# A 128-row second product in the split attention scores of a hybrid encoder kernel

## The chip, the cores and the metric

The kernel runs on one core of one Trainium2 chip. The metric is the device time of one execution in microseconds, as the median of several executions.

## The reference, cut to what matters

Two layers, each with one combined input projection whose columns feed differential attention (8 heads of two softmax maps), multi-head latent attention (8 heads) and a gate; then one output projection onto the residual. There are 512 frames and 2048 channels, all in 32-bit floats.

```python
for l in range(DEPTH):                       # DEPTH = 2
    h = _rmsnorm(x, norm_g[l])
    proj = einsum('bsd,de->bse', h, w_in[l])
    dq, dk, dv, cq, ckv, kr, gate = split(proj)
    # differential attention: for each block of 128 queries, for each map m
    #   s = q_m k_m^T * 64**-0.5 + bias ;  p = softmax(masked s)
    #   o = (p_1 - lam * p_2) v,   then an RMSNorm per head
    # latent attention: s = (q_nope k_nope^T + q_rope k_rope^T) * 192**-0.5
    y = concatenate([o_a, o_b], -1) * silu(gate)
    x = x + einsum('bse,ed->bsd', y, w_out[l])
return _rmsnorm(x, final_norm_g)
```

A block of queries reads only the keys up to its own end, so a score is 128 x w with w = 128, 256, 384 or 512.

## The kernel before, in words

Products that must keep 32-bit accuracy are made of parts. A value is split into a high part, rounded to the type fp32r that TensorE multiplies at full rate, and a low part, the rest. The projections use three products (high x high, high x low, low x high), all in `mm3` (line 249). Weights come in units of 512 KB: `emit_dma` loads one into one of two raw buffers, `emit_split` (lines 195, 196) makes the high part on ScalarE (`whi`) and the low part on VectorE (`wlo`), into four buffers each. `touch` issues the splits up to two units ahead of the unit in use.

The scores of differential attention have only 64 rows to sum over for each map. `split_stack` (lines 484, 486) therefore writes q for map m as 128 rows: the high part in the map's own half, the low part in the other half. `evac_qk` writes the high part of k into both halves and the low part of k, `kl`, into the map's own half only (lines 742 to 745). `mm_stack` then makes a score of two products: one over 128 rows with the high part of k (line 492), which gives high x high and low x high at once, and one over the 64 rows of the map's own half with the low part of k (line 493). `diff_scores` calls it for both maps of a head. `mla_scores` calls it once, behind a plain 32-bit product (line 523); its rotary key has high and low parts in both halves already, as `lat_kr` transposes a doubled copy. So in each layer 8 heads x 4 blocks x 2 maps, and 8 heads x 4 blocks, run through lines 492 and 493.

Every engine works off its instructions in the order in which the program issues them. `mix` puts the attention steps of one group of two heads (`pend`) between the projection pieces of the next group. Within a group a pipeline runs: in each slot the scores of one block, the transposes of an earlier block's probabilities (line 309, tiles `pT`), then the products with v (lines 573 and 620), each one or two slots behind. `evac_qk` stands at the end of each QK group, eight times in all. Small per-row statistics live in the pool `st`, and the low parts of k in the pool `kl`.

Of the kernel before, what the change touches and what calls it, by code (L numbers as in the profile page):

```python
# [11 lines left out]
F32 = mybir.dt.float32  # L12
F32R = mybir.dt.float32r
AF = mybir.ActivationFunctionType
ALU = mybir.AluOpType
AX = mybir.AxisListType

P = 128
S = 512
# [12 lines left out]
BUCKETS = 32  # L32
MAX_DIST = 128
MAPS = 16
# [3 lines left out]
NVEC = 640  # L38
# [16 lines left out]
def tile_hybrid_trunk(ctx, tc, x, norm_g, w_in, diff_lambda, diff_subln_g, mla_q_norm_g,  # L55
                      mla_w_q_b, mla_kv_norm_g, mla_w_kv_b, w_out, rel_bias, final_norm_g,
                      onehot, cos2, sin1, out):
    nc = tc.nc
# [4 lines left out]
    def pool(name, bufs, space=None):  # L63
        kw = {} if space is None else {"space": space}
        return ctx.enter_context(tc.tile_pool(name=name, bufs=bufs, **kw))

    const = pool("const", 1)
    big = pool("big", 16)
# [6 lines left out]
    bip = pool("bias", 2)  # L75
    tp = pool("tmp", 4)
    op = pool("o", 2)
    stp = pool("st", 16)
    keep = pool("keep", 4)
    krp = pool("kr", 1)  # L80
    klp = pool("kl", 3)
    pj = pool("pj", 4, bass.MemoryType.PSUM)
    at = pool("at", 4, bass.MemoryType.PSUM)
    dr = pool("dr", 1, bass.MemoryType.DRAM)
# [1 line left out]
    def B(shape, dtype, name):  # L86
        return big.tile(shape, dtype, tag="B", name=name)

    def T(name, pl=None, tag="T"):
        return (pl or tp).tile([P, 512], F32, tag=tag, name=name)  # L90

    def stat(name):
        return stp.tile([P, 8], F32, tag="st", name=name)

    def bank(name):
        return at.tile([P, 512], F32, tag="at", name=name)

    def acopy(out, in_, scale=1.0):
        nc.scalar.activation(out, in_, AF.Copy, scale=scale)  # L99
# [117 lines left out]
    def group(ids, nb, mm, evac, order=None, ahead=2, cost=4):  # L217

        banks = {}
        left = {u: nb for u, _, _ in ids}  # L220
        seen = dict.fromkeys(range(nb), 0)
        kt = ids[-1][1] + ids[-1][2]
        if order is None:
            order = [(i, b) for i in range(len(ids)) for b in range(nb)]

        def piece(i, b):
            u, k0, n = ids[i]
            hi, lo = touch(u, ahead)
            if b not in banks:
                banks[b] = pj.tile([P, 512], F32, tag="pj", name="pj")  # L230
            for k in range(n):
                mm(banks[b], b, hi, lo, k, k0 + k, seen[b] == 0, seen[b] == kt - 1)
                seen[b] += 1
            left[u] -= 1
            if left[u] == 0:
                finish(u)
            if seen[b] == kt:
                evac(b, banks.pop(b))

        return [(ids[i][2] * cost, lambda i=i, b=b: piece(i, b)) for i, b in order]  # L240
# [10 lines left out]
    def mm_T(act):  # L251

        def mm(bk, b, hi, lo, k, kb, first, last):
            c = slice(b * P, (b + 1) * P)
            mm3(bk, (hi[:, k, c], lo[:, k, c]), act(kb), True, first, last)
        return mm

    def mm_S(act, w):

        def mm(bk, b, hi, lo, k, kb, first, last):  # L260
            c = slice(b * P, (b + 1) * P)
            ahi, alo = act(kb)
            mm3(bk[:, :w], (hi[:, k, :w], lo[:, k, :w]), (ahi[:, c], alo[:, c]), False, first, last)
        return mm
# [52 lines left out]
    with tc.manual_schedule():  # L317
# [12 lines left out]
        for q in range(4):  # L330
            load_x(x, 0, q)

        gsrc = const.tile([46, P], F32, name="gsrc")
        sp.dma_start(out=gsrc[0:32], in_=norm_g.rearrange("l (k p) -> (l k) p", p=P))
        sp.dma_start(out=gsrc[32:40], in_=mla_q_norm_g.rearrange("l (k p) -> (l k) p", p=P))
        sp.dma_start(out=gsrc[40:44], in_=mla_kv_norm_g.rearrange("l (k p) -> (l k) p", p=P))
# [5 lines left out]
        cosT = const.tile([P, NSB, ROPE], F32, name="cosT")  # L342
        sinT = const.tile([P, NSB, ROPE // 2], F32, name="sinT")
        dlam = B([P, DEPTH, 2, 2, DH], F32, "dlam")
        relb = const.tile([BUCKETS, MAPS], F32, name="relb")
        oneh = big.tile([BUCKETS, NVEC], F32, tag="B", name="oneh")
        def load_small():
            sp.dma_start(out=relb, in_=rel_bias)
            sp.dma_start(out=oneh, in_=onehot)
            sp.dma_start(out=cosT, in_=cos2.rearrange("(b p) c -> p b c", p=P))  # L350
            sp.dma_start(out=sinT, in_=sin1.rearrange("(b p) c -> p b c", p=P))
            sp.dma_start(
                out=dlam.rearrange("p l a b d -> p (l a b d)"),
                in_=diff_lambda.rearrange("l a d -> (l a d)").unsqueeze(0).to_broadcast([P, DEPTH * 4 * DH]),
            )
# [122 lines left out]
        def half(m):  # L478
            return slice(m * DH, (m + 1) * DH)

        def split_stack(bk, dst, scale=1.0):

            for m in range(2):
                acopy(dst[half(m), m, :], bk[half(m)], scale=scale)
            for m in range(2):
                nc.vector.scalar_tensor_tensor(
                    out=dst[half(1 - m), m, :], in0=bk[half(m)], scalar=scale, in1=dst[half(m), m, :].bitcast(F32),
                    op0=ALU.mult, op1=ALU.subtract)

        def mm_stack(dst, q, khi, klo, m, first):  # L490

            nc.tensor.matmul(dst, lhsT=q[:, m], rhs=khi, start=first, stop=False)  # L492
            nc.tensor.matmul(dst, lhsT=q[half(m), m], rhs=klo[half(m)], start=False, stop=True)  # L493

        def diff_scores(l, hd, qb, bt, st_):
            w = (qb + 1) * P
            mx, sm = stat("mx"), stat("sum")
            s = []
            for m in range(2):
                bk = bank("sc")  # L500
                mm_stack(bk[:, :w], hd["qk"][:, 0, :, qb * P:(qb + 1) * P], hd["qk"][:, 1, m, :w], hd["kl"][:, :w], m, True)
                sm_t = T("s", smp, "sm")
                nc.vector.tensor_tensor_reduce(  # L503
                    out=sm_t[:, :w], in0=bk[:, :w], in1=bt[:, m, 512 - w:512], op0=ALU.add, op1=ALU.max,
                    scale=1.0, scalar=LOW, accum_out=mx[:, m:m + 1])
                s.append(sm_t)
            nc.vector.tensor_scalar(out=mx[:, 2:4], in0=mx[:, 0:2], scalar1=-1.0, scalar2=None, op0=ALU.mult)  # L507
            for m in range(2):
                nc.scalar.activation(s[m][:, :w], s[m][:, :w], AF.Exp, bias=mx[:, 2 + m:3 + m], accum_out=sm[:, m:m + 1])  # L509
            nc.vector.reciprocal(sm[:, 2:4], sm[:, 0:2])  # L510
            nc.vector.scalar_tensor_tensor(out=sm[:, 4:5], in0=sm[:, 3:4], scalar=neglam[:, l:l + 1], in1=sm[:, 0:1],
                                           op0=ALU.mult, op1=ALU.mult)
            nc.vector.scalar_tensor_tensor(out=s[0][:, :w], in0=s[1][:, :w], scalar=sm[:, 4:5], in1=s[0][:, :w],
                                           op0=ALU.mult, op1=ALU.add)
            st_["p"], st_["rc"] = s[0], sm[:, 2:3]
# [125 lines left out]
        for l in range(DEPTH):  # L641
# [88 lines left out]
            for i in range(4):  # L730
                qk, v = {}, {}

                def evac_qk(b, bk, qk=qk):
                    if b < 2:
                        qk[b] = {"qk": B([P, 2, 2, S], F32R, "qk")}
                        split_stack(bk, qk[b]["qk"][:, 0], DH ** -0.5)
                        return
                    hd = qk[b - 2]
                    hd["kl"] = klp.tile([P, S], F32R, tag="kl", name="kl")
                    k = hd["qk"][:, 1]  # L740
                    for m in range(2):
                        acopy(k[half(m), m], bk[half(m)])
                    for m in range(2):
                        acopy(k[half(1 - m), m], bk[half(m)])
                        nc.vector.tensor_tensor(hd["kl"][half(m)], bk[half(m)], k[half(m), m].bitcast(F32), op=ALU.subtract)

                def evac_v(b, bk, v=v):
                    if "t" not in v:
                        v["t"] = vp.tile([P, NSB, 256], F32, tag="v", name="v")
                    (nc.vector.tensor_copy if b % 2 else acopy)(v["t"][:, b, :], bk[:, :256])  # L750

                pieces = []
                if i:
                    pieces += group(g["G", i - 1], 2, mm_T(ah), evac_gate(2 * i - 2))
                pieces += group(g["V", i], NSB, mm_S(ah, 256), evac_v, cost=2)
                pieces += group(g["QK", i], 4, mm_T(ah), evac_qk)
                mix(pieces, pend, MIX_DIFF)
                pend = diff_items(l, i, qk, v, gate_y)
# [311 lines left out]
```

## Time and profile before

| | |
|---|---|
| three runs | 1833.92, 1834.45, 1834.63 us (median 1834.45) |
| profiled execution | 1835.62 us, span of the instructions 1833.8 us |
| granted TensorE clock, mean | 0.997 of full speed |
| TensorE matmuls busy | 1804.4 us, 98% of the span, 9245 instructions |
| weight loads busy (beside the matmuls) | 1492.3 us, 81% |
| VectorE, ScalarE, GpSimd busy | 952.9, 710.1, 32.2 us |
| memory traffic | 179.34 MB, mean 98 GB/s |

Times in the profile's rows are microseconds from the start of the span. PE is TensorE's matmuls, PEld its weight loads, DVE is VectorE, ACT is ScalarE. Matmuls run in a pipeline, so the duration of one is longer than the distance to the next; distances between starts tell the rate. "issue" as the reason for idle time means that the profile shows nothing that the engine waited for.

### The profile page before, as it was taken

What the parts mean: (1) busy time and instruction counts of PE and PEld (TensorE: products, weight loads), DVE (VectorE), ACT (ScalarE), POOL (GpSimd) and SP (SyncE); (2) the same over time, 40 slices, a digit from 0 to 9 for tenths busy, and PEclk for the clock granted to TensorE, in tenths of its full rate; (3) what the DMA queues carried; (4) which work ended last, traced back from release to release, by engine and by line L of the source; (5) the groups of instructions that cost most, each with busy time, mean ns of one, the idle gap of its engine ahead of it and who ended that gap; (6) DMA issues with size and microseconds to landing.
All of it is one profiled execution on the core that took longest, in us unless ns stands there. A gap on an engine that the chain in (4) does not pass through costs nothing.

```text
span 1833.8 us, 23481 instructions
## 1 busy us (share of the span) xinstructions
PE 1804.4 (98%) x9245; PEld 1492.3 (81%) x9245; DVE 952.9 (52%) x1753; ACT 710.1 (39%) x1424; POOL 32.2 (2%) x53
## 2 busy tenths in 40 slices
PE   6999999999999999999999999999999999999997
PEld 4888888887878987878879887888887798878786
DVE  5426445453646774454362353644545667645554
ACT  5324444443443442333352343444443344433333
POOL 1000000000000000000000000000000000000000
PEclk9999999999999999999999999999999999999999
DMA  5543232232322431313333232323223224213223
GB/s 173 173 144 98 72 101 81 71 114 70 115 81 78 118 104 58 115 58 103 127 105 102 71 114 71 114 71 102 81 70 115 80 81 149 70 58 113 71 92 126
DMA packets 142330, 179.34 MB, mean 98 GB/s; under 512 B 16942, under 2 KB 94812, under 8 KB 142092
## 3 DMA queue, kind: packets, MB, share of 16 engines
q1 hardware_dynamic: 142220, 177.85, 31.7%
q8 instruction: 72, 1.18, 0.3%
q14 instruction: 38, 0.31, 0.1%
HBM read 169.39 MB, written 13.67 MB: 100 GB/s over the span
## 4 chain that ended last, share of the span: by engine, by line
PE 97%; ACT 1%; DVE 1%; issue 0%; DMA 0%; POOL 0%; SPq 0%; ACTq 0%; POOLq 0%; DVEq 0%
PE pj L249 81%; PE sc L493 4%; PE sc L492 2%; PE pT L309 2%; PE sc L523 2%; PE oT L620 2%; PE ov L573 2%; PE nT L309 1%; PE oT L309 0%; ACT xn L99 0%; PE cT L309 0%; ACT whi L195 0%; DMA xs<-in_x 0%; DVE nt L457 0%; POOL rs L314 0%
## 5 line engine op out<-in xcount | busy, mean ns | idle before, releaser
L196 DVE TENSOR_TENSOR wlo<-raw,whi 128x1024 fp32r<-128x1024 f32 (+1 forms) x272 | 327.7, 1211 | 323.9 <-ACT whi L195 316.5
L249 PE MATMUL pj<-hThi,whi 128*128 128x512 f32 x1024 | 413.6, 404 | 0.0
L249 PE MATMUL pj<-hThi,wlo 128*128 128x512 f32 x1024 | 400.0, 391 | 0.0
L249 PE MATMUL pj<-hTlo,whi 128*128 128x512 f32 x1024 | 399.5, 390 | 0.0
L195 ACT ACTIVATE whi<-raw 128x1024 fp32r<-128x1024 f32 (+1 forms) x272 | 282.6, 1047 | 180.6 <-PE pj L249 106.3
L249 PE MATMUL pj<-whi,yhl 128*128 128x512 f32 x1024 | 326.8, 400 | 0.0
L249 PE MATMUL pj<-whi,hThi 128*128 128x256 f32 (+2 forms) x768 | 243.1, 317 | 2.1 <-ACT hThi L99 2.1
L249 PE MATMUL pj<-whi,hTlo 128*128 128x256 f32 (+2 forms) x768 | 236.2, 308 | 0.0
L249 PE MATMUL pj<-wlo,hThi 128*128 128x256 f32 (+2 forms) x768 | 236.0, 307 | 0.0
L249 PEld LDWEIGHTS pj<-hThi,whi 128*128 128x128 f32 x1024 | 192.5, 188 | 43.3 <-issue 4.3
L249 PEld LDWEIGHTS pj<-hThi,wlo 128*128 128x128 f32 x1024 | 192.2, 188 | 41.4
L249 PEld LDWEIGHTS pj<-hTlo,whi 128*128 128x128 f32 x1024 | 192.8, 188 | 35.1
L249 PEld LDWEIGHTS pj<-whi,yhl 128*128 128x128 f32 x1024 | 184.3, 188 | 38.6 <-issue 3.5
L249 PE MATMUL pj<-wlo,yhl 128*128 128x512 f32 x512 | 200.5, 392 | 0.0
L509 ACT ACTIVATE s<-s,mx 128x128 f32<-128x128 f32 (+3 forms) x128 | 71.1, 557 | 294.0 <-DVE mx L507 294.0
L249 PEld LDWEIGHTS pj<-whi,hThi 128*128 128x128 f32 x768 | 147.2, 192 | 10.5 <-ACT hThi L99 2.5
L249 PEld LDWEIGHTS pj<-whi,hTlo 128*128 128x128 f32 x768 | 147.3, 192 | 5.5 <-DVE hTlo L462 0.7
L249 PEld LDWEIGHTS pj<-wlo,hThi 128*128 128x128 f32 x768 | 147.0, 191 | 5.6
L720 DVE RECIPROCAL ge<-ge 128x256 f32<-128x256 f32 x64 | 112.2, 1753 | 2.2
L249 PEld LDWEIGHTS pj<-wlo,yhl 128*128 128x128 f32 x512 | 96.1, 188 | 20.9
L503 DVE CUSTOM_DVE_ANT_0 s<-sc,bt 128x128 f32<-128x128 f32 (+3 forms) x128 | 59.7, 486 | 100.3 <-POOL bt L413 56.2
L529 ACT ACTIVATE s<-sc,mx 128x128 f32<-128x128 f32 (+1 forms) x64 | 33.8, 529 | 156.5 <-DVE mx L527 156.5
(153 smaller groups left out, 1876.1 us busy)
## 6 DMA issues: line engine op xcount, KB each, us to landing
raw<-in_w_in SPq DMA_DIRECT2D x112, 512.0 KB, 3.8
raw<-in_w_in SPq DMA_DIRECT2D x128, 256.0 KB, 2.9
raw<-in_w_out SPq DMA_DIRECT2D x64, 512.0 KB, 3.7
xs<-in_x SPq DMA_DIRECT2D x32, 256.0 KB, 5.3
bt<-btab SPq DMA_DIRECT2D x16, 512.0 KB, 5.4
btab<-vecd SPq DMA_DIRECT2D x16, 320.0 KB, 6.6
raw<-in_w_in SPq DMA_DIRECT2D x10, 480.0 KB, 3.7
raw<-in_mla_w_q_b SPq DMA_DIRECT2D x16, 256.0 KB, 3.2
```

Of the source, the lines that this page charges most:

```text
L195: nc.scalar.activation(hi[:, :n], raw[:, :n], AF.Copy)
L196: nc.vector.tensor_tensor(lo[:, :n], raw[:, :n], hi[:, :n].bitcast(F32), op=ALU.subtract)
L249: nc.tensor.matmul(dst, lhsT=a, rhs=b, start=first and t == 0, stop=last and t == 2)
L309: nc.tensor.transpose(dst, src, ident)
L492: nc.tensor.matmul(dst, lhsT=q[:, m], rhs=khi, start=first, stop=False)
L493: nc.tensor.matmul(dst, lhsT=q[half(m), m], rhs=klo[half(m)], start=False, stop=True)
L503: nc.vector.tensor_tensor_reduce(out=sm_t[:, :w], in0=bk[:, :w], in1=bt[:, m, 512 - w:512], op0=ALU.add, op1=ALU.max, scale=1.0, scalar=LO ...
L509: nc.scalar.activation(s[m][:, :w], s[m][:, :w], AF.Exp, bias=mx[:, 2 + m:3 + m], accum_out=sm[:, m:m + 1])
L523: nc.tensor.matmul(bk[:, :w], lhsT=qk[:, par, q], rhs=qk[:, 2 + par, :w], start=True, stop=False)
L573: nc.tensor.matmul(bk[:, :P], lhsT=st_["pt"][:, kb * P:(kb + 1) * P], rhs=v["t"][:, kb, hp * P:(hp + 1) * P], start=kb == 0, stop=kb == qb)
L620: nc.tensor.matmul(o_["bk"][:, qb * P:(qb + 1) * P], lhsT=v["t"][:, kb, hp * P:(hp + 1) * P], rhs=st_["pt"][:, kb * P:(kb + 1) * P], start ...
L720: nc.vector.reciprocal(e[:, c], e[:, c])
```

## The change

The second product of `mm_stack` takes all 128 rows of q (the high part in the map's own half, the low part in the other) and meets a `kl` that holds the low part of k in both halves. So the score also contains low x low. `evac_qk` writes the low part of each map twice, once into each half, and `kl` gets a plane for each map. The buffer is twice as wide and there are two instead of three. To make room, the pool of statistics has 14 tiles instead of 16, the gathered gains use a temporary tile, and the small relative-bias table lies behind its one-hot table in one tile.

```diff
-    stp = pool("st", 16)
+    stp = pool("st", 14)
...
-    klp = pool("kl", 3)
+    klp = pool("kl", 2)
...
-        gsrc = const.tile([46, P], F32, name="gsrc")
+        gsrc = T("gsrc")[:46, :P]
...
-        relb = const.tile([BUCKETS, MAPS], F32, name="relb")
-        oneh = big.tile([BUCKETS, NVEC], F32, tag="B", name="oneh")
+        relo = big.tile([BUCKETS, NVEC + MAPS], F32, tag="B", name="oneh")
+        oneh, relb = relo[:, :NVEC], relo[:, NVEC:]
...
             nc.tensor.matmul(dst, lhsT=q[:, m], rhs=khi, start=first, stop=False)
-            nc.tensor.matmul(dst, lhsT=q[half(m), m], rhs=klo[half(m)], start=False, stop=True)
+            nc.tensor.matmul(dst, lhsT=q[:, m], rhs=klo, start=False, stop=True)
...
-                mm_stack(bk[:, :w], hd["qk"][:, 0, :, qb * P:(qb + 1) * P], hd["qk"][:, 1, m, :w], hd["kl"][:, :w], m, True)
+                mm_stack(bk[:, :w], hd["qk"][:, 0, :, qb * P:(qb + 1) * P], hd["qk"][:, 1, m, :w], hd["kl"][:, m, :w], m, True)
...
-                    hd["kl"] = klp.tile([P, S], F32R, tag="kl", name="kl")
+                    hd["kl"] = klp.tile([P, 2, S], F32R, tag="kl", name="kl")
                     k = hd["qk"][:, 1]
                     for m in range(2):
                         acopy(k[half(m), m], bk[half(m)])
                     for m in range(2):
                         acopy(k[half(1 - m), m], bk[half(m)])
-                        nc.vector.tensor_tensor(hd["kl"][half(m)], bk[half(m)], k[half(m), m].bitcast(F32), op=ALU.subtract)
+                        for n in (m, 1 - m):
+                            nc.vector.tensor_tensor(hd["kl"][half(n), m], bk[half(m)], k[half(m), m].bitcast(F32), op=ALU.subtract)
```

## Rows read from the trace of the kernel before

**Rows 1.** The page: busy time by engine (us, share, instructions), and the chain by line.

```profile
PE 1804.4 (98%) x9245; PEld 1492.3 (81%) x9245; DVE 952.9 (52%) x1753; ACT 710.1 (39%) x1424; POOL 32.2 (2%) x53
...
PE pj L249 81%; PE sc L493 4%; PE sc L492 2%; PE pT L309 2%; PE sc L523 2%; PE oT L620 2%; PE ov L573 2%; PE nT L309 1%; PE oT L309 0%; ACT xn L99 0%; PE cT L309 0%; ACT whi L195 0%; DMA xs<-in_x 0%; DVE nt L457 0%; POOL rs L314 0%
```

**Rows 2.** Waits of the weight loads: us in total, times, longest us.

```profile
PEld sc L493 <- issue: 41.3, 138, 0.6
```

**Rows 3.** Order of time, TensorE, a score over 512 keys: start, us, engine, line, operation.

```profile
218.27 0.39 PE L249 MATMUL pj<-hTlo,whi 128*128 128x512 f32 x1
...
219.18 0.19 PEld L492 LDWEIGHTS sc<-qk 128*128 128x128 f32 x1
219.40 0.39 PE L492 MATMUL sc<-qk 128*128 128x512 f32 x1
219.72 0.18 PEld L493 LDWEIGHTS sc<-kl,qk 64*128 64x128 f32 x1 [0.35 <-issue]
...
220.14 0.19 PEld L492 LDWEIGHTS sc<-qk 128*128 128x128 f32 x1 [0.24 <-issue]
...
220.57 0.18 PEld L493 LDWEIGHTS sc<-kl,qk 64*128 64x128 f32 x1 [0.25 <-issue]
...
221.00 0.19 PEld L249 LDWEIGHTS pj<-hThi,whi 128*128 128x128 f32 x1 [0.25 <-issue]
...
221.11 0.19 PEld L249 LDWEIGHTS pj<-hTlo,whi 128*128 128x128 f32 x1
...
221.34 0.40 PE L249 MATMUL pj<-hTlo,whi 128*128 128x512 f32 x1
```

**Rows 4.** Order of time, TensorE, differential scores over 128 and 256 keys.

```profile
154.53 0.22 PE L492 MATMUL sc<-qk 128*128 128x128 f32 x1
...
155.78 0.40 PE L249 MATMUL pj<-hTlo,whi 128*128 128x512 f32 x1
...
198.72 0.28 PE L492 MATMUL sc<-qk 128*128 128x256 f32 x1
...
200.20 0.39 PE L249 MATMUL pj<-hTlo,whi 128*128 128x512 f32 x1
```

**Rows 5.** Order of time, TensorE, latent scores over 512 and 128 keys.

```profile
703.76 1.02 PE L523 MATMUL sc<-qkm 128*128 128x512 f32 x2
704.19 0.19 PEld L492 LDWEIGHTS sc<-krT,qrT 128*128 128x128 f32 x1 [0.24 <-issue]
...
705.93 0.40 PE L249 MATMUL pj<-wlo,yhl 128*128 128x512 f32 x1
...
672.92 0.38 PE L523 MATMUL sc<-qkm 128*128 128x128 f32 x2
...
673.89 0.39 PE L249 MATMUL pj<-cqlo,whi 128*128 128x512 f32 x1
```

**Rows 6.** Order of time, TensorE, undisturbed projection products of 256 columns.

```profile
685.45 0.28 PE L249 MATMUL pj<-wlo,ckvhl 128*128 128x256 f32 x1
...
685.57 0.40 PE L249 MATMUL pj<-whi,ckvhl 128*128 128x256 f32 x2
...
685.80 0.28 PE L249 MATMUL pj<-wlo,ckvhl 128*128 128x256 f32 x1
```

**Rows 7.** Groups by line and form (mean ns, idle), and the end of the first QK group.

```profile
L486 DVE SCALAR_TENSOR_TENSOR qk<-pj,qk 64x512 fp32r<-64x512 f32 x32 | 22.0, 689 | 24.5 <-ACT qk L99 24.0
L745 DVE TENSOR_TENSOR kl<-pj,qk 64x512 fp32r<-64x512 f32 x32 | 22.0, 689 | 19.1 <-ACT qk L99 19.1
...
148.84 0.69 DVE L745 TENSOR_TENSOR kl<-pj,qk 64x512 fp32r<-64x512 f32 x1 [0.66 <-ACT qk L99]
...
149.79 2.36 DVE L196 TENSOR_TENSOR wlo<-raw,whi 128x1024 fp32r<-128x1024 f32 x2 [0.25 <-ACT whi L195]
```

**Rows 8.** Order of time, a softmax's last step and the transposes that read it.

```profile
750.28 0.49 DVE L531 TENSOR_SCALAR s<-s,sum 128x512 f32<-128x512 f32 x1
...
753.52 0.60 PE L309 MATMUL pT<-ident,s 128*128 128x128 f32 x4
```

## The prediction, made before the change was built

> **What bounds the kernel now.** I read the page's busy shares and its chain that ended last first. TensorE is busy 98% of the span and the chain is TensorE nearly throughout, 81% of it the projection products of line 249; VectorE works 52% and ScalarE 39% [rows 1]. So only what shortens TensorE's own sequence can shorten the kernel by much, and work put on VectorE is free as long as nothing waits for it. A busy matmul row says little about how fast matmuls follow each other, so the next view is the list of waits of the weight loads. Its largest entry is the change's own line: the loads of line 493 stood idle 41.3 us in 138 cases, with no releaser that the profile knows [rows 2]. Then I read the order of time around one score.
>
> In a row of projection products of 512 columns each load starts together with the matmul ahead of it, and the starts are (219.40 − 218.27) / 5 = 0.226 us apart [rows 3]. The load of the first score product does the same: it starts at 219.18, and its matmul at 219.40. The load of the second product, the one over 64 rows, does not: it starts at 219.72, when the 0.226 us of the product ahead are over, and its idle of 0.35 us is what the list of waits added up. The load after it, over 128 rows again, starts late too (220.14), and so do the two after that (220.57, 221.00). Only the load at 221.11 is back in step. The reader should see four loads in a row that lie bare, each next to a step between 128 and 64 rows, and none elsewhere.
>
> **The price of a step.** I count from the start of the first score matmul to the start of the second matmul behind the score, because the delay ends only there, and set against it the same matmuls at their undisturbed distances. An undisturbed 512-column product takes 0.226 [rows 3], one of 256 columns (685.80 − 685.45) / 3 = 0.117 [rows 6]. For 128 columns no undisturbed row exists: a quarter of 0.226 gives 0.057, and two loads that nothing holds apart start 0.11 apart (221.00, 221.11) [rows 3]. Since each product brings its own load I take 0.11, with 0.057 as the other end.
> - Differential score, 512 keys: 221.34 − 219.40 = 1.94 against 5 x 0.226 = 1.13, so 0.81 us lost [rows 3].
> - 256 keys: 200.20 − 198.72 = 1.48 against 4 x 0.117 + 0.226 = 0.69, so 0.79 lost; 128 keys: 155.78 − 154.53 = 1.25 against 4 x 0.11 + 0.226 = 0.67, so 0.58 lost (0.80 with the other end) [rows 4]. For 384 keys I take 0.80, between its neighbours.
> - Latent score, 512 keys: one step into 64 rows and one out. The 32-bit product ahead is two instructions; the next load starts 0.43 after it began [rows 5], so 0.86 for both. From 703.76 to 705.93 it is 2.17 against 0.86 + 4 x 0.226 = 1.76, so 0.41 lost: half of the differential loss, as half the steps should give. 128 keys: 673.89 − 672.92 = 0.97 against 4 x 0.11 + 0.226 = 0.67, so 0.30 lost [rows 5]. For 256 and 384 keys I take 0.41.
>
> **What the change removes.** The second product of each pair becomes a 128-row one, so no score leaves the 128-row form; the number of matmuls and loads stays. There are 2 layers x 8 heads = 16 differential and 16 latent scores of each width (line 493's matmuls are 128 and 64). Differential: 16 x (0.58 + 0.79 + 0.80 + 0.81) = 47.7 us. Latent: 16 x (0.30 + 3 x 0.41) = 24.5 us; here nothing else changes, because the low part of the rotary key is already written for both halves. Sum 72.2 us. With 0.057 for 128 columns it would be 16 x (4 + 2) x 0.053 = 5 us more. The other bound, 0.117 as for 256 columns, takes under 1 us off.
>
> [...]
>
> **What it adds.** In the evacuation of k, VectorE does four subtractions a head instead of two: 32 more of 689 ns [rows 7], 22 us in all. They write across halves; the split of q does the same at the same 689 ns, so crossing costs nothing. They come in 8 places, the ends of the QK groups, four in each, 2.8 us. ScalarE's copy of the second half waits for the subtractions of the first (same bank), so its queue is late too, by 1.4 to 2.8 us, and behind it stand the copies that split the next weights. Who needs these? The last subtraction ends at 148.84 + 0.69 = 149.5, and the first score reads k at 154.53, 5.0 us later [rows 4, 7]; 2.2 us are left. The two weight splits queued behind end at 152.15 [rows 7] and would end near 155. A split is issued two units ahead of the one that TensorE starts on, and a unit is 24 products, 5.4 us, so its first use comes near 149 + 11 = 160. Without that cover the bill would be at most 8 x 2.8 = 22 us. I enter zero.
>
> A score that comes earlier could let the next wait show. The transposes of the probabilities need the softmax, and between the two stand at most two scores, 0.8 us each. The shortest of the 128 distances from a finished softmax (750.28 + 0.49) to its transposes (753.52) is 2.75 us [rows 8]. Zero again.
>
> The pools: two buffers for kl instead of three (of twice the width) suffice, since a group's scores are over long before the next group's k is evacuated, at the group's end. Fourteen statistics tiles instead of sixteen hold what is live (per score two, kept for at most three slots of the pipeline, and two sums of squares). The gains in a temporary tile and the relative bias beside its one-hot table are read once at the start; their transfers stay where they are in the queue. All at zero, with 0 to 3 us at the high end.
>
> **The rivals.**
> - *The pair still stalls*: both products now use the very same weights, and the second load might have to wait for the first product. Then the load inside each pair stays bare and the one behind it is free: half the gain, 36 us, 1798. Against it: the projections load one weight tile twice running, and the three products around it take 0.117 each [rows 6].
> - *It does not do what it says*: the bare loads come from something else in line 493 (its moving operand, its bank), and the 128-row product keeps them. Then 1834 to 1838. For it: the profile names no releaser [rows 2]. Against it: the delay also stands at loads of lines 492 and 249 that touch neither [rows 3], and the latent score loses half as much with half the steps [rows 5].
> - *The gain turns into waits*: TensorE gets 72 us less time in the attention stretches, and softmax, splits or weight transfers come last instead. With a fifth given back, 1777. Against it: the margins above and VectorE's 52%.
> - *Slower*: the longer evacuation of k holds up the first score of the next heads. It happens at 8 places, so each microsecond past the 5.0 us margin costs 8 us, and it decides from 72.2 / 8 = 9 us, that is, if a chain is longer by 14 us. At 16 us it gives 1762 + 8 x 11 = 1850. For it: ScalarE and VectorE take turns on one bank. Against it: I find 2.8 us, not 14.
>
> **How the numbers follow.** The profiled execution took 1835.62 us; minus 72.2 that is 1763.4. The median, 1.2 us below it, becomes 1762.3, 3.9% less. Its own range is 1755 to 1768. Chances: forecast 0.80, pair still stalls 0.07, waits 0.06, no effect 0.04, slower 0.03. The range 1752 to 1783 takes in the two ends for 128 columns, the 3 us of the pools and most of the third rival, and leaves out some 0.15. About 0.2% is what a measurement of this kernel can tell from no change; faster by more than that 0.93, within it 0.04, slower 0.03.
>
> **What would show it.** After the change no load has 64 rows; the 41.3 us of waits of line 493's loads are gone; a 512-key differential score goes through in 5 x 0.226 us; VectorE's busy time grows by 22 us to about 975; TensorE still fills 98%. The prediction is wrong if loads of 128 rows inside the pairs start only after the matmul ahead, if 128-column products follow at other than 0.11, or if TensorE's waits for kl, the probabilities or wlo come up.

## The result

The changed kernel takes 1766.99 us (median of four runs, 1766.37 to 1767.19); the kernel before took 1834.54 beside it. The ratio is 0.9631, with a 95% interval of 0.9614 to 0.9648: 67.6 us, 3.7% faster. The forecast was 1762.3 us, its range 1752 to 1783. The profiled executions, 1835.62 and 1766.37 us, lie 69.25 us apart, because that of before was 1.1 us over its median and that of after 0.6 us under.

The page of the changed kernel, its span and its busy times (us, share, instructions), answers to [rows 1]:

```profile
span 1764.6 us, 23519 instructions
...
PE 1735.2 (98%) x9245; PEld 1486.4 (84%) x9245; DVE 970.0 (55%) x1785; ACT 703.3 (40%) x1424; POOL 32.0 (2%) x53
```

TensorE has as many instructions as before, 69 us less of busy time and the same 98%: its own sequence became shorter, and it still sets the end. VectorE has the 32 more instructions. The list of waits of the weight loads (us in total, times, longest) answers to [rows 2]:

```profile
PEld sc L492 <- issue: 3.8, 16, 0.2
PEld sc L493 <- issue: 3.8, 16, 0.2
...
PEld pT L309 <- ACT s L529: 0.5, 2, 0.2
```

The 41.3 us of line 493 are down to 3.8. What is left in lines 492 and 493 are 16 times 0.24 us each, in the latent scores over 512 keys, which stand behind the two-instruction 32-bit product, and none of it is a change of form. No load waits for `kl` or `wlo`, and the transposes of the probabilities wait 0.5 us in all.

A differential score over 512 keys in order of time (start, us, engine, line, operation), answering to [rows 3], and below it the first one over 128 keys, answering to [rows 4]:

```profile
213.72 0.39 PE L492 MATMUL sc<-qk 128*128 128x512 f32 x1
213.72 0.19 PEld L493 LDWEIGHTS sc<-kl,qk 128*128 128x128 f32 x1
213.94 0.40 PE L493 MATMUL sc<-kl,qk 128*128 128x512 f32 x1
...
214.18 0.40 PE L492 MATMUL sc<-qk 128*128 128x512 f32 x1
...
214.42 0.39 PE L493 MATMUL sc<-kl,qk 128*128 128x512 f32 x1
...
214.65 0.39 PE L249 MATMUL pj<-hThi,whi 128*128 128x512 f32 x1
...
214.88 0.40 PE L249 MATMUL pj<-hTlo,whi 128*128 128x512 f32 x1
```

```profile
153.84 0.22 PE L492 MATMUL sc<-qk 128*128 128x128 f32 x1
...
154.52 0.39 PE L249 MATMUL pj<-hTlo,whi 128*128 128x512 f32 x1
154.53 0.19 PEld L249 LDWEIGHTS pj<-hThi,wlo 128*128 128x128 f32 x1
```

The load of line 493 now has 128 rows and starts at 213.72 together with the product ahead of it. From the first score product to the second projection product it is 214.88 − 213.72 = 1.16 us, where it was 1.94; over 128 keys 154.52 − 153.84 = 0.68 against 1.25.

The gain can be read off the order of time as a whole. These are, in the changed kernel, the last transposes of a differential head and the first latent score of the first layer, and the first transposes of the next layer's norm; then the two of the kernel before that are not among the rows ahead.

```profile
575.72 0.60 PE L309 MATMUL oT<-ident,o 128*128 128x128 f32 x4
...
649.29 0.38 PE L523 MATMUL sc<-qkm 128*128 128x128 f32 x2
...
881.14 1.05 PE L309 MATMUL nT<-ident,xn 128*128 128x128 f32 x6 [0.18 <-ACT xn L99]
```

```profile
599.38 0.60 PE L309 MATMUL oT<-ident,o 128*128 128x128 f32 x4
...
916.07 1.16 PE L309 MATMUL nT<-ident,xn 128*128 128x128 f32 x7 [0.18 <-ACT xn L99]
```

Differential: 599.38 − 154.53 = 444.85 us before [rows 4] and 575.72 − 153.84 = 421.88 after, 22.97 us for eight heads, or 2.87 for a set of four widths. Latent: 916.07 − 672.92 = 243.15 before [rows 5] and 881.14 − 649.29 = 231.85 after, 11.30 for eight heads, 1.41 for a set. With 16 sets of each that is 45.9 + 22.6 = 68.5 us. The first score starts 0.7 us earlier, before any score has run; together 69.2, which is the difference of the spans, 1833.8 − 1764.6.

### The profile page after: what moved, and what is told of

Its sections match the earlier page's. It is cut to its first block, busy times and chain, and to the rows that moved or that the text cites. A ratio compares the mean times of both kernels' runs of the same rounds, so it can differ in the third digit from the quotient of the medians.

```text
span 1764.6 us, 23519 instructions
## 1 busy us (share of the span) xinstructions
PE 1735.2 (98%) x9245; PEld 1486.4 (84%) x9245; DVE 970.0 (55%) x1785; ACT 703.3 (40%) x1424; POOL 32.0 (2%) x53
## 3 DMA queue, kind: packets, MB, share of 16 engines
q8 instruction: 72, 1.18, 0.3%
## 4 chain that ended last, share of the span: by engine, by line
PE 97%; ACT 1%; DVE 1%; DMA 1%; issue 0%; POOL 0%; SPq 0%; ACTq 0%; POOLq 0%; DVEq 0%
PE pj L249 84%; PE oT L620 2%; PE ov L573 2%; PE pT L309 2%; PE sc L523 2%; PE sc L493 2%; PE sc L492 2%; PE nT L309 1%; DMA xs<-in_x 1%; PE oT L309 0%; PE cT L309 0%; ACT xn L99 0%; DVE nt L457 0%; ACT whi L195 0%; ACT junk L424 0%
```

## Experiments

**The latent scores alone.** The kernel before, with

```diff
-            nc.tensor.matmul(dst, lhsT=q[half(m), m], rhs=klo[half(m)], start=False, stop=True)
+            r = slice(0, P) if not first else half(m)
+            nc.tensor.matmul(dst, lhsT=q[r, m], rhs=klo[r], start=False, stop=True)
```

> The kernel before, with the second product over 128 rows in the 64 latent scores alone; k, the pools and the 128 differential scores stay as they were. Theory (each step between 64 and 128 rows costs about 0.2 us and nothing else matters): the latent part of the gain by itself, 16 x 1.42 = 22.7 us as the trace of the changed kernel has it, so 1834.5 - 22.7 = 1811.8 us, VectorE unchanged at 953 us busy, and the differential scores still 0.8 us too long. Rival (the gain comes mostly from the pools, the order of memory or the start): clearly less than 10 us, above 1824.

Measured: 1811.78 us beside 1834.94 for the kernel before, ratio 0.9875 (0.9859 to 0.9892), 23.2 us less. The waits of the loads (the line is now 494):

```profile
PEld sc L494 <- issue: 26.1, 106, 0.4
```

So a change of two slices, with no work added anywhere and no pool touched, brings the latent third of the gain. The waits that are left, 26.1 us, belong to the differential scores. The pools and the start are not where this third comes from.

**Half the steps, the same 64-row products.** The kernel before, with the products of a differential score in another order:

```diff
...
             for m in range(2):
-                bk = bank("sc")
-                mm_stack(bk[:, :w], hd["qk"][:, 0, :, qb * P:(qb + 1) * P], hd["qk"][:, 1, m, :w], hd["kl"][:, :w], m, True)
+                nc.tensor.matmul(bks[m][:, :w], lhsT=q[:, m], rhs=hd["qk"][:, 1, m, :w], start=True, stop=False)
+            for m in range(2):
+                nc.tensor.matmul(bks[m][:, :w], lhsT=q[half(m), m], rhs=hd["kl"][half(m), :w], start=False, stop=True)
...
```

> The kernel before, with all its 64-row products, but in a differential score the first products of both maps run first and the second products of both maps behind them: two changes between 128 and 64 rows in a score instead of four, the same loads and products. Theory (the change of form is what costs): half of the differential gain, 16 x 2.86 / 2 = 22.9 us, so 1811.6 us; the load of the second 64-row product, which goes to the other half of the rows, runs beside the product ahead. Rival (every 64-row load lies bare, wherever it stands, and the 128-row load behind one too): three bare loads of four are left, a gain of 11.4 us, 1823 us. Second rival (the loads are bare because both products of a pair write one bank): all are hidden, 1789 us.

Measured: 1802.86 us, ratio 0.9825 (0.9810 to 0.9839), 32.1 us less. That is none of the three: 9 us better than half the steps should give, 14 us short of no bare load at all. A score over 512 keys in order of time (x2 stands for two instructions of the kind), and below it one 64-row product of the kernel before:

```profile
177.05 0.63 PE L502 MATMUL sc<-qk 128*128 128x512 f32 x2
177.61 0.19 PEld L504 LDWEIGHTS sc<-kl,qk 64*128 64x128 f32 x2 [0.36 <-issue]
177.61 0.50 PE L504 MATMUL sc<-kl,qk 64*128 64x512 f32 x2
178.04 0.19 PEld L249 LDWEIGHTS pj<-whi,hThi 128*128 128x128 f32 x1 [0.25 <-issue]
...
178.27 0.28 PE L249 MATMUL pj<-whi,hTlo 128*128 128x256 f32 x1
```

```profile
219.72 0.49 PE L493 MATMUL sc<-kl,qk 64*128 64x512 f32 x1
```

Two loads lie bare, one at the step into 64 rows (177.61) and one at the step out of it (178.04). That much is as the theory has it. But between the two, in 0.43 us, stand both 64-row products, where in the kernel before one alone took 0.42 (219.72 to 220.14) [rows 3]. They sum over different halves of the rows, and they run side by side: from the start of the first to the end of the second it is 0.50 us, where one alone lasts 0.49, and in the score over 256 keys at 196.71 it is 0.38, where one alone in the kernel before lasts 382 ns on average. The whole, from 177.05 to 178.27, is 1.22 us; four products one after the other and a projection product of 256 columns are 4 x 0.226 + 0.117 = 1.02, two steps are 0.4, so 1.42 were due, and 0.2 is missing, one product. Over a set of four widths that makes 0.11 + 0.117 + 0.17 + 0.226 = 0.62 us, 16 x 0.62 = 10 us, and 22.9 + 10 = 33 is near the 32.1 measured. So the step is what costs, and two 64-row products next to each other have a merit of their own that the kernel before never used.

**Everything but the 128-row product.** The changed kernel, with its pools, its wide kl and its 64 subtractions, but

```diff
-            nc.tensor.matmul(dst, lhsT=q[:, m], rhs=klo, start=False, stop=True)
+            nc.tensor.matmul(dst, lhsT=q[half(m), m], rhs=klo[half(m)], start=False, stop=True)
```

> The changed kernel with its pools, its doubled low part of k and all 64 subtractions, but the second products go over 64 rows again as before. Theory (the added work on VectorE and the pools are covered): 1834.5 us within 1.5 us, perhaps 0.7 us less as the first score of the changed kernel came 0.7 us earlier before any score had run; VectorE busy 970 us. Rival (part of the 4.7 us by which the forecast was too low is the price of the added subtractions or of the smaller pools): 1836 to 1840 us.

Measured: 1835.86 us beside 1834.94, ratio 1.0005 (0.9996 to 1.0014): no difference that the runs can tell. Busy times and the wait of line 493:

```profile
PE 1805.1 (98%) x9245; PEld 1492.5 (81%) x9245; DVE 974.3 (53%) x1785; ACT 708.7 (39%) x1424; POOL 32.0 (2%) x53
...
PEld sc L493 <- issue: 41.3, 138, 0.6
```

The 41.3 us of waits are back in full, and VectorE's 974.3 us, 21 more than before, cost nothing that shows: the interval runs from 0.7 us less to 2.6 us more. So it rules out that the added work is the whole of the 4.7 us by which the forecast was too low, and not that it is some of it; that the changed kernel has no wait for `kl` or `wlo` and 0.5 us of waits for probabilities (the result) speaks against it. The 0.7 us of the earlier start aren't here either (the first score starts at 154.59), so they don't come from the pools or the wider `kl`.

**The subtractions doubled.** The changed kernel, with

```diff
-                        for n in (m, 1 - m):
+                        for n in (m, 1 - m, m, 1 - m):
```

> The changed kernel, with each subtraction for the low part of k done twice: 64 more of 0.69 us, 5.5 us at the end of each QK group. Theory (the cover is nearly used up: in the changed kernel the low part of k is ready 2.9 us before the first score, and the bias tile of the first head, queued behind the raw weights, lands late enough that the first transposes have 0.6 to 2.5 us left): TensorE waits about 3 us at each of the 8 places, 24 us, 1791 us, between 1780 and 1800. Rival (VectorE idles 45% of the time, so added work there is free): 1767 us.

Measured: 1809.35 us, ratio to the kernel before 0.9863 (0.9848 to 0.9879): 42 us slower than the changed kernel, where the theory had 24 and at most 1800 us. VectorE's idle share bought nothing, so the rival falls, and the theory had the size wrong. The waits of the weight loads that were not there before, then the third of the eight places in order of time:

```profile
PEld pj L249 <- DVE wlo L196: 25.0, 10, 2.9
...
PEld pT L309 <- DVE s L513: 9.6, 7, 2.7
```

```profile
367.35 2.87 DVE L746 TENSOR_TENSOR kl<-pj,qk 64x512 fp32r<-64x512 f32 x4 [0.66 <-ACT qk L99]
...
367.50 0.22 PE L492 MATMUL sc<-qk 128*128 128x128 f32 x1
...
371.53 0.79 PE L249 MATMUL pj<-hThi,wlo 128*128 128x512 f32 x1 [2.48 <-DVE wlo L196]
...
372.12 0.63 PE L249 MATMUL pj<-hThi,whi 128*128 128x512 f32 x1
...
373.82 0.63 PE L249 MATMUL pj<-hTlo,whi 128*128 128x512 f32 x1
```

The first score does not wait: it starts at 367.50, while the last subtractions run until 370.22. TensorE waits 2.48 us for the low part of the next weights, as it does at each of the eight places, and here what follows is slow: the starts at 372.12 and 373.82 are four products apart, 0.425 us each instead of 0.226. The granted clock (the column behind the five engines) behind this wait, and behind the same wait at the first place:

```profile
371.00:372.00 1.00, 0.47 (x1) 0.47 (x2) 1.00 (x2) 0.00 (x0) 0.00 (x0) 0.50 0.00 0
372.00:374.00 2.00, 2.00 (x6) 1.52 (x6) 0.61 (x1) 0.00 (x0) 0.00 (x0) 0.50 0.60 134
```

```profile
156.99 0.50 PE L249 MATMUL pj<-hThi,wlo 128*128 128x512 f32 x1 [2.49 <-DVE wlo L196]
...
157.00:159.00 2.00, 2.00 (x9) 1.63 (x10) 1.07 (x1) 0.00 (x0) 0.00 (x0) 1.00 0.38 61
```

From 371 to 374 it is 0.50. The products come 0.42 to 0.43 us apart there, and 0.22 to 0.24 again from 374.53 on: some seven products at 0.2 us more, 1.4 us. At 156.99 the same wait leaves it at 1.00. Behind four of the eight waits some products come 0.42 to 0.43 us apart; behind the other four they come, from the second on, 0.22 to 0.24 us apart. Both kernels issue the same 9245 matmuls in the same order, so the delay can be read off matmul by matmul: the eight places cost 5.6, 5.9, 5.3, 4.9, 5.1, 5.5, 5.7 and 5.2 us, 43 us in all, and make the whole difference. The four with the slower products (5.9, 5.3, 5.5, 5.7) cost 0.4 us more on average than the others, and not 1.4, because the waits that follow, mostly of the first transposes for the softmax, are shorter. So a place costs what was added there, 5.5 us: nearly nothing was left to cover it. VectorE at 55% is not free.

**No second product.** The kernel before, with line 493 left out. The part high x low is missing from its scores.

```diff
-            nc.tensor.matmul(dst, lhsT=q[:, m], rhs=khi, start=first, stop=False)
-            nc.tensor.matmul(dst, lhsT=q[half(m), m], rhs=klo[half(m)], start=False, stop=True)
+            nc.tensor.matmul(dst, lhsT=q[:, m], rhs=khi, start=first, stop=True)
```

> The kernel before without the second product of any score (the part high x low of the scores is left out; k's low part is still made). Theory: what goes is the 64-row product's own time, which is that of its columns (0.11 + 0.117 + 0.172 + 0.226 = 0.63 us a set of four widths, 48 sets, 30 us), and all the steps between forms, 68.5 us as the changed kernel's trace has them: 1834.9 - 98.5 = 1736 us, and 30 us below the changed kernel. Rival (the bare loads belong to the scores as such, whatever the form of their products): only the products' own time goes, 1804 us.

Measured: 1734.77 us beside 1835.45, ratio 0.9455 (0.9441 to 0.9469), 100.7 us less, where the theory had 98.5. The second products cost 100 us over 64 rows and 32 over 128 (1766.99 − 1734.77), and 30 is the time of their columns as the expectation adds it up. Two thirds of their price were the steps.

**The changed kernel in the other order.** First products of both maps, then second products:

```diff
...
             for m in range(2):
-                bk = bank("sc")
-                mm_stack(bk[:, :w], hd["qk"][:, 0, :, qb * P:(qb + 1) * P], hd["qk"][:, 1, m, :w], hd["kl"][:, m, :w], m, True)
+                nc.tensor.matmul(bks[m][:, :w], lhsT=q[:, m], rhs=hd["qk"][:, 1, m, :w], start=True, stop=False)
+            for m in range(2):
+                nc.tensor.matmul(bks[m][:, :w], lhsT=q[:, m], rhs=hd["kl"][:, m, :w], start=False, stop=True)
...
```

> The changed kernel, but in a differential score the first products of both maps run first and then the second products, so that no weight tile is loaded twice running. Theory (a second load of the same weights waits for nothing): 1767 us within 1 us, all loads hidden as in the changed kernel. Rival (part of the 4% by which a set of scores fell short of its forecast, 0.12 us of 2.98, is the load of weights that are in use): up to 16 x 0.12 = 2 us less, 1765 us.

Measured: 1766.15 us (1765.33 to 1767.27), ratio to the kernel before 0.9627 (0.9611 to 0.9643), against 0.9631 (0.9614 to 0.9648) for the changed kernel. The two can't be told apart, and 2 us lie within the interval, so the times alone do not settle the rival. The traces do for the most part: score by score, a set of four widths takes 0.03 us less than in the changed kernel, a quarter of the 0.12 us that the rival wants. Loading one weight tile twice running costs next to nothing here: without it the median is 0.84 us lower, 0.05 a set, and no load of a differential score stands in the list of waits either way.

## Why the prediction was right, and where it was not

**The bare loads and their cause.** Right. Where the text says that no load lies bare elsewhere, it is too strong: the load at 704.19, behind the 32-bit product of a latent score, lies bare too [rows 5], 16 of these are left after the change, and they were not in the sum. The four bare loads of a score were the steps between 128 and 64 rows: they go with the form (the result), come back with it alone (41.3 us in the third experiment), and halve with the steps (the second). The rival that the pair still stalls falls with the load at 213.72, the rival without effect with the result, and the rival that the gain turns into waits with the list of waits: 0.5 us for probabilities, none for weights.

**The terms of the sum.** Right in kind, 5% too large: 72.2 us forecast, 68.5 measured by sets. A set of differential scores brought 2.87 instead of 2.98. Score by score, up to the next score, the four widths brought 0.56, 0.76, 0.76 and 0.77, where 0.58, 0.79, 0.80 and 0.81 were entered. One reason shows in the rows of 512 columns: the products follow each other there at 0.23 to 0.24 us (213.94, 214.18, 214.42, 214.65) and not at the 0.226 of an undisturbed row (an fp32r product; the plain 32-bit one of as many columns takes 2 x 0.43 = 0.86 [rows 5]). I set the disturbed case against the smoothest row of the trace; a row from beside the scores would have been the fairer one. For 128 keys the bound by the loads held: 0.68 us against 0.67 forecast, so 0.11 and not 0.057 a product. A set of latent scores brought 1.41 instead of 1.53, and each width a little less than entered: 0.27, 0.39, 0.38 and 0.39 for 0.30, 0.41, 0.41 and 0.41. Over 512 keys a score takes 679.51 − 677.73 = 1.78 against 1.76. A third or so of the difference is a case that I did not look at: where transposes and not a projection stand behind the score, less was lost to begin with. Such a score over 384 keys, before and then after; the last two lines are the one of after over 512 keys:

```profile
698.65 0.81 PE L523 MATMUL sc<-qkm 128*128 128x384 f32 x2
...
700.57 0.40 PE L249 MATMUL pj<-wlo,yhl 128*128 128x512 f32 x1
```

```profile
672.96 0.81 PE L523 MATMUL sc<-qkm 128*128 128x384 f32 x2
...
674.52 0.40 PE L249 MATMUL pj<-wlo,yhl 128*128 128x512 f32 x1
...
677.73 1.02 PE L523 MATMUL sc<-qkm 128*128 128x512 f32 x2
...
679.51 0.40 PE L249 MATMUL pj<-wlo,yhl 128*128 128x512 f32 x1
```

Before, it took 700.57 − 698.65 = 1.92 us, after, 674.52 − 672.96 = 1.56, so 0.36 gained where I entered 0.41.

Of the 4.7 us between the forecast of 1762.3 and the median of 1766.99, the sum makes 3.7, the earlier start takes 0.7 off, and the rest is that the profiled execution, from which I counted, lay 1.2 us over its median before and 0.6 us under it after.

**The added work at zero.** The value was right as far as the third experiment can tell, but three steps to it were wrong, the margin was far smaller than the text had it, and that it just sufficed was luck. Rows of after, then of before: the end of the first QK group and the first head's softmax (the last two rows of after are the same softmax and load at the third place).

```profile
149.54 1.40 DVE L746 TENSOR_TENSOR kl<-pj,qk 64x512 fp32r<-64x512 f32 x2 [0.66 <-ACT qk L99]
...
150.97 2.36 DVE L196 TENSOR_TENSOR wlo<-raw,whi 128x1024 fp32r<-128x1024 f32 x2
...
152.22 1.50 SPq L182 DMA_DIRECT2D raw<-in_w_in  x2
...
153.78 0.50 SPq L410 DMA_DIRECT2D bt<-btab  x1
...
159.73 0.20 POOL L413 MEMSET bt<- 64x128 f32 x1 [126.63 <-DMA bt<-btab]
...
162.08 0.35 DVE L513 SCALAR_TENSOR_TENSOR s<-s,sum 128x128 f32<-128x128 f32 x1
...
162.77 0.14 PEld L309 LDWEIGHTS pT<-ident,s 128*128 128x128 f32 x1
...
365.23 0.35 DVE L513 SCALAR_TENSOR_TENSOR s<-s,sum 128x128 f32<-128x128 f32 x1
...
365.64 0.14 PEld L309 LDWEIGHTS pT<-ident,s 128*128 128x128 f32 x1
```

```profile
145.67 0.69 DVE L745 TENSOR_TENSOR kl<-pj,qk 64x512 fp32r<-64x512 f32 x1 [0.66 <-ACT qk L99]
...
155.78 0.19 PEld L249 LDWEIGHTS pj<-hThi,wlo 128*128 128x128 f32 x1
...
158.78 0.20 POOL L413 MEMSET bt<- 64x128 f32 x1 [125.06 <-DMA bt<-btab]
...
161.13 0.35 DVE L513 SCALAR_TENSOR_TENSOR s<-s,sum 128x128 f32<-128x128 f32 x1
...
164.75 0.14 PEld L309 LDWEIGHTS pT<-ident,s 128*128 128x128 f32 x1
```

The step on the first score took the last subtraction for the one that it reads. That one belongs to the second head of the group; the first score reads the first head's, ready at 145.67 + 0.69 = 146.4, 8.2 us ahead. So the place named for the slower rival was no danger, and the fourth experiment shows it: with 5.5 us more the first score still did not wait (367.50).

The step on the weight splits put the first use of the late unit near 160. The load of its low part starts at 154.53, right behind the first score. The first of the two splits is done at 150.97 + 1.18 = 152.15, 2.4 us ahead; in the kernel before it was done near 151.0 and used at 155.78, 4.8 us ahead. I had taken "two units ahead" for two whole units of time; as I read it now, the split's place in ScalarE's queue behind the copies of k had used one of them up already. The lateness was smaller than entered, too: measured from the first score the splits start 153.84 − 150.97 = 2.9 us ahead, where it was 154.53 − 149.79 = 4.7 [rows 4, 7], so they are 1.9 us later and not 2.8; one of the four new subtractions filled idle time of VectorE (it idled 1.13 us ahead of its third subtraction before, and 0.42 ahead of the third pair after).

The step on the softmax looked for scores between it and the transposes, and found at most 0.8 us for each. It missed that the first softmax of a group starts with a transfer: the bias tile is issued by the queue that carries the raw weights, behind loads that wait for the splits (152.22, then 153.78). It is there at 159.73 instead of 158.78, while TensorE comes to the transposes earlier. Their cover, from the end of the softmax (162.43) to the load (162.77), is 0.34 us, where it was 164.75 − 161.48 = 3.3. At the third place it is 365.64 − 365.58 = 0.06, and at six of the eight under 0.9, where no place had less than 3.0 before. The rule that I applied, count what is queued behind the lengthened work, was not followed to its end: the queue behind the split is SyncE's. The fourth experiment shows what lay past the margin. The slower rival had the price right, about 8 us for each microsecond past the margin (42 us for 5.5), but neither the wait nor the margin: what comes late is the weights' low part and the softmax, and of the second kind hardly anything was left.

**Loads over all rows, and the step.** Loads over all 128 rows run beside the products here: that of the second score product starts together with the first product (213.72), and the next product follows 0.22 us later. The step costs about 0.2 us (0.15 over 128 keys) [rows 3, 4, 5], and in the second experiment none stands between the two 64-row products: 0.43 us for both. Why a step takes this time no run shows.

## What to carry to other kernels

Look for matmuls of another row count in the midst of 128-row ones: a step in and a step out cost 0.4 us here from 256 columns on and 0.3 at 128. Filling the missing rows with something useful was worth 3.7% of a kernel that was 98% busy, and standing the 64-row products of a differential score together 1.75%. When work is added on an engine with time to spare, follow each queue behind it to the consumer, transfers included, and write down the margin that is left and not only that there is one. An undisturbed distance for the sum is best taken from rows next to the disturbed place.

## What the runs showed of the hardware beyond that

Two 64-row products on different halves of the rows run side by side: 0.43 us for both at 512 columns with one step, where one alone took 0.42 [rows 3]. In the fourth experiment eight waits of TensorE of 2.48 us each were followed in four cases by some products 0.42 to 0.43 us apart, with a granted clock of 0.50 at the one place where it was read (371 to 374), and in the other four by products 0.22 to 0.24 us apart, with a clock of 1.00 at the first of them (157 to 159). At the third place the fall slowed some seven products by 1.4 us in all, but a place with slower products cost only 0.4 us more on average than one without, as the wait behind it was shorter.
